# A float32 transformer with split weights: its memory pools opened in another order

## The chip, the cores and the metric

The kernel runs on one core of a Trainium2 chip. The metric is the device time of one execution in microseconds (us), the median of several runs.

## The reference

Two transformer blocks of two layers each work on one sequence of 256 tokens, 1024 features wide, in float32. The first block has in each layer a gated feed-forward, a mixer (window attention beside a gated convolution, then a gated recurrence) and a second gated feed-forward, each behind an RMS norm. The second block has norms that are scaled and shifted by a modulation, a mixer of three kinds of attention, and a dense feed-forward in its first layer; in its second layer a mixture of eight experts, of which each token takes two. Most of the arithmetic is the product of 256 tokens with large weights:

```python
def _swiglu(x, wg, wu, wd):
    return (jax.nn.silu(x @ wg) * (x @ wu)) @ wd      # wg, wu: 1024 x 2816, wd: 2816 x 1024
...
    for e in range(N_EXPERTS):
        out = out + gates[..., e:e + 1] * _swiglu_2(h, w_gate[e], w_up[e], w_down[e])
```

## The kernel before

**Products.** TensorE (PE) multiplies in float32r. To keep float32 accuracy, each operand is split into two float32r parts, a high one and a low one, and a product is the sum of three matmuls: high by high, low by high, high by low (`mm3`, lines 334, 335 and 337). In nearly all of them the activations, transposed, are the stationary operand (`lhsT`, 128 x 128, in a slot), and a row tile of a weight, 512 or 256 columns wide, is the moving operand (`rhs`). `fmajor` (line 595) has it the other way round: 128 columns of a weight are stationary, and both token tiles of the activations, 2 x 128 columns, move. The experts with few tokens put the two parts of 64 tokens side by side in one stationary operand, so that two matmuls do (line 429).

**Weights.** `load` (line 300) brings a piece of a weight, mostly 128 partitions x 2048 columns (1 MB), from DRAM into one of four `raw` tiles, on SP's queue. `split` (line 306) makes the two parts of each half of it: ScalarE (ACT) copies 1024 columns to a `wh` tile in float32r (by way of `act`, line 222), and VectorE (DVE) subtracts that from `raw` into a `wl` tile (by way of `tt`, line 231). There are eight `wh` and eight `wl` tiles of 4 KB per partition. In the feed-forwards of the first block and the dense one, one or two slots (`ext`) serve as a ninth and tenth pair. The feed-forwards go through their 2816 hidden columns in six chunks: up products of a chunk, the gate, the transpose of the hidden columns (line 457), the down products into accumulators `acc`.

**Pools.** `K.__init__` opens the pools one after the other, and each begins where the one before it ends. Every tile is rounded up to 32 bytes per partition. In the order of before:

- `cst`, the constants: `x0` and `x1` (4096 bytes per partition each), `ident` and `ones` (512 each), `fold` (32), `mhalf` (64), `cols` (1600), `consts` (3744), `sincos` (512), together 15168 bytes. It begins at byte 16512 = 129 x 128 of each partition.
- `raw`, four tiles of 8192 bytes; `wh` and `wl`, eight of 4096 bytes each.
- `sm`, small tiles of 4 to 512 bytes, together 5152 bytes.
- `slots`: `s8` of 4096 bytes and eleven more of 8192: activations, their split transposes, gains, hidden columns, attention.

Two pools outside SBUF follow, `ps` (PSUM) and `dr` (DRAM). Which tile serves which step, the order of the instructions and the queues are set by the rest of the program, which names pools and tags and no addresses.

**The experts** (`moe`): the tokens are sorted into seven places, the largest expert's chunks run beside the others' by a plan (`plan`), and 264 pieces of weights are loaded for them. `scatter` (line 1579) multiplies in plain float32.

Of the kernel before, what the change touches and what calls it, by code (L numbers as in the profile page):

```python
# [20 lines left out]
# where each chunk's parts begin in a packed feed-forward  # L21
# [4 lines left out]
# ---------------------------------------------------------------- host layout  # L26
# [63 lines left out]
def pack(inp):  # L90
    a = {}
# [4 lines left out]
    # even mixer: conv value and gate by halves, queries by pairs of heads that use different keys, keys and values  # L96
    w = inp["even_w_in"][0]
# [7 lines left out]
    # odd mixer: half of the gate, recurrence, the rest of the gate  # L105
    w = inp["odd_w_in"][0]
# [6 lines left out]
    # per-feature vectors, features on partitions  # L113
# [15 lines left out]
    r = inp["moe_router_2"][0]  # L129
# [3 lines left out]
    # per-feature vectors as rows  # L133
# [5 lines left out]
    # modulation: 6 segments of 1024 a layer, outputs on partitions  # L139
# [4 lines left out]
    # second mixer: [q latent, kv latent, rope key], [band q, band k], [stick q, stick k], [stick v, band v]  # L144
# [19 lines left out]
    # constants of the shapes  # L164
# [27 lines left out]
# ---------------------------------------------------------------- device  # L192
class K:
    def __init__(self, ctx, tc, A, out, dbg=None):
        self.tc, self.nc, self.A, self.out, self.dbg = tc, tc.nc, A, out, dbg or {}
        e = ctx.enter_context
        self.cst = e(tc.tile_pool(name="cst", bufs=1))
        self.raw_p = e(tc.tile_pool(name="raw", bufs=4))
        self.h_p = e(tc.tile_pool(name="wh", bufs=8))
        self.l_p = e(tc.tile_pool(name="wl", bufs=8))  # L200
        self.sm_p = e(tc.tile_pool(name="sm", bufs=1))
        self.slots = e(tc.tile_pool(name="slots", bufs=1))
        self.ps = e(tc.tile_pool(name="ps", bufs=4, space=bass.MemoryType.PSUM))
        self.dr = e(tc.tile_pool(name="dr", bufs=1, space=bass.MemoryType.DRAM))
        self.n = 0
        self.ext, self.turn, self.in_moe, self.c_row = (), 0, False, None
        self.first, self.behind = True, None
        self.setup()

    # --- small helpers  # L210
# [13 lines left out]
    def warm(self, func, after):  # L224
        """has the scalar engine load a function's table behind one of its instructions"""
        t = self.small("mx", 2, bufs=1)[:, 0:1]
        with self.tc.issue_after(after.ins):
            return self.act(t, self.ones[:, 0:1], func)
# [27 lines left out]
    def setup_late(self):  # L256
        """what the first products don't need"""
# [20 lines left out]
    def begin(self, ins):  # L278
        """the first norms' steps keep their order"""
        return self.pin(ins) if self.first else ins  # L280
# [16 lines left out]
    # --- weights: raw piece from DRAM, split exactly into two float32r parts  # L297
# [8 lines left out]
    def split(self, raw, nk, n, pin=False):  # L306
        """nk row tiles by n columns: a list over row tiles of the (hi, lo) views [128, n]"""
# [21 lines left out]
    def mm3(self, out, xs, ws, first, last):  # L329
        """out += x.T @ w over pairs; xs, ws lists of (hi, lo) operands"""  # L330
# [8 lines left out]
    def mm3_groups(self, out, xs, groups, c0, n, first, last):  # L339
        """the same over groups of row tiles, columns c0:c0 + n of each"""  # L340
# [6 lines left out]
    def rstd(self, ss, n, eps, tag="r"):  # L347
        """1 / sqrt(ss + eps)"""
# [17 lines left out]
    def stat(self, t, h, gain=None):  # L366
        """mean squares of one half of a token tile; with a gain, of the product too, which is kept"""
# [25 lines left out]
    def split_T(self, xT, t, src, groups=(0, 1)):  # L393
        """src [128 tokens, 1024] -> the two parts of its transpose, [128, token tile, 8, 128]"""
# [25 lines left out]
    # --- gated feed-forward  # L420
    def prod(self, out, xs, groups, c0, n, first, last, half=False):
        """out += x.T @ w. Half: the two parts of 64 tokens lie side by side in x, and their products land in
        the two halves of the partitions"""
# [20 lines left out]
    def glu_T(self, u, n, h, l, half=False):  # L444
        """the two parts of the transpose; of half a tile side by side in h"""
# [15 lines left out]
    def ffn(self, src, base, xk, tiles, finish, side=None, tick=None, ext=(), defer=None, hl=(2, 3), bufs=None, half=False, hook=None, head=None):  # L461
# [65 lines left out]
        def down_w(c):  # L527
            """groups of row tiles and their first column, for each half of the output"""
# [50 lines left out]
    # --- feature-major projection: columns of w on partitions, both token tiles in the free axis  # L579
    def fmajor(self, out, xT, groups, c0, n=128):  # L580
        """out [n, 256] = (x @ w[:, c0:c0 + n]).T"""
# [15 lines left out]
    def tmajor(self, out, xT, t, groups, c0, n):  # L597
        """out [128 tokens, n] = x @ w[:, c0:c0 + n]"""
# [3 lines left out]
    def in_block(self, src, off, n):  # L602
        """the row tiles of one block of n columns of a 1024-row weight"""
# [34 lines left out]
    # --- softmax attention of one query tile; score banks hold heads side by side  # L638
    def softmax_av(self, nk, banks, p_sb, pt_sb, values, o, rinv, sinks=None, scale=None):
        """banks: (psum view [128, heads, nk * 128], head ids); o [128, heads * 64] psum; rinv [128, heads]"""  # L640
# [39 lines left out]
    # --- first block, layer 0: window attention beside a gated convolution  # L680
    def even_mixer(self, xT, finish, defer):
        nc, A = self.nc, self.A
        src = A["ew_in"]
        # bias of each head by distance, skewed through DRAM: A[p, j] = r[p + j], p = 127 - query
# [20 lines left out]
        # keys and values, a token tile at a time  # L705
# [34 lines left out]
        # depthwise convolution over time  # L740
# [7 lines left out]
        # attention  # L748
# [26 lines left out]
        # the last channels by products with the taps on a diagonal  # L775
# [14 lines left out]
        # norm over channels, by sums over partitions that land on all of them  # L790
# [29 lines left out]
    def decay(self):  # L820
        """4 log sigmoid(lam), and its negative; halves of the gates' biases"""
# [26 lines left out]
    # --- first block, layer 1: gated linear recurrence  # L848
    def odd_mixer(self, xT, finish, defer):
# [9 lines left out]
        # half of the gate, a token tile at a time  # L859
# [12 lines left out]
        def gates(g, b):  # L872
            """twice the sigmoid less one"""
# [43 lines left out]
        def pre(b, n=1):  # L917
            sl = slice(2 * b, 2 * (b + n))
            # 1 - a^2 = tanh(-log a) (1 + a^2)
# [51 lines left out]
    # --- second block: modulation of both layers, spread over the first block's products  # L971
# [63 lines left out]
    def final_norm_mod(self, t, shift, gain, xT):  # L1035
        """the norm between the blocks, then the modulated one, of the product that stat kept"""
# [12 lines left out]
    def rope_tables(self):  # L1049
# [17 lines left out]
        for which, quarter in ((0, 0.0), (1, 0.25)):  # L1067
            # nearest whole turn, then the rest in three exact steps
# [10 lines left out]
        # [sin | sin] -> [-sin | sin]  # L1079
        self.ts(self.sc[:, 0, :, 0:16], self.sc[:, 0, :, 0:16], -1.0)  # L1080

    def rope(self, out, src, t, nh, tmp):
        """out, src [128, nh, 32]; src in psum"""
# [8 lines left out]
    def band_tables(self):  # L1092
        """band bias of both layers: edge value, then the table, in DRAM to be read skewed"""
# [9 lines left out]
    def mixer(self, l, xT, finish, defer):  # L1103
# [14 lines left out]
        # latents of the low-rank attention, normed, transposed  # L1118
# [11 lines left out]
        for t, p in enumerate(pa):  # L1130
# [13 lines left out]
            # the key part that turns, shared by the heads, and its share of their mean squares  # L1144
# [9 lines left out]
        # stick-breaking queries and keys, feature-major  # L1154
# [7 lines left out]
        # band attention's queries and keys: normed a head, transposed by pairs  # L1162
# [16 lines left out]
        # up-projections, rope, keys normed a head (a query's norm goes into the softmax's scale), transposes  # L1179
# [51 lines left out]
        # stick-breaking: keys on partitions; log weights are z - sum of softplus from the key up to the query  # L1231
# [29 lines left out]
        # values of both  # L1261
# [10 lines left out]
        def stick():  # L1272
            # the sums over the keys behind, the weights and their products with the values
# [28 lines left out]
        # band attention  # L1302
        def band(t):
# [13 lines left out]
            # places in order of (j, i); head 2 i + j  # L1317
# [7 lines left out]
        # low-rank attention  # L1325
# [49 lines left out]
    # --- experts: tokens gathered by one-hot products, 128 to a slot  # L1375
# [8 lines left out]
    def logits(self, t, xT):  # L1384
        """router logits of one token tile; the parts of the router side by side"""
# [8 lines left out]
    def moe(self, h, res, xT, defer):  # L1394
# [5 lines left out]
        # the first expert's first hidden columns, for every token: its products run beside the routing  # L1400
# [18 lines left out]
        # rank of each expert for a token: larger logit first, then lower index  # L1419
# [12 lines left out]
        # place of each token in its expert's list, from 1 (0: not in it), and the experts' counts on all partitions  # L1432
# [11 lines left out]
        def tables(one, kinds, pcol):  # L1444
            """one-hot of place by token for each token tile; kinds: the first place of each 128 rows, and whether
            they are 64 places twice, for the two parts"""
# [9 lines left out]
        def gather(one, kinds, outs, alone=False):  # L1456
            """the two parts of the gathered tokens, transposed; a half's side by side"""
# [23 lines left out]
        def turned(one, oneT, nb, gcol):  # L1481
            """the one-hots transposed, and each place's gate"""
# [13 lines left out]
        def make(got, i, m, half, pcol, gcol):  # L1496
            """fills got with what an expert's slot needs; m has room for the one-hots and their transposes"""
# [29 lines left out]
        # expert 0 has the first slot; the others follow by count: room for 192 tokens, 128 (three) and 64 (three)  # L1527
# [13 lines left out]
        # one-hot [slot, expert]  # L1541
# [21 lines left out]
        # tokens that no slot has room for  # L1563
# [8 lines left out]
        def scatter(parts):  # L1572
            """parts of the product that carries places back to tokens, added to x"""
# [9 lines left out]
        def expert(src, got, out, **kw):  # L1583
            """the tokens of one slot"""
# [17 lines left out]
        # the expert with the most tokens: 128 and 64 more, a chunk of its products beside each later expert's  # L1602
# [78 lines left out]
        def head():  # L1681
            """the places' part of the first hidden columns, transposed"""
# [10 lines left out]
        # when each chunk of the largest expert is done: most beside the experts of 64  # L1693
# [58 lines left out]
def emit(tc, A, out, dbg=None):  # L1752
    with ExitStack() as ctx:
# [6 lines left out]
        def prep(name):  # L1760
            """the norm in front of a part, for one token tile at a time"""
# [94 lines left out]
# ---------------------------------------------------------------- launch  # L1856
# [15 lines left out]
```

## Time and profile before

| | |
|---|---|
| median of 3 runs | 2288.79 us |
| lowest and highest | 2286.12 and 2289.21 us |
| span of the profiled execution (first to last instruction) | 2284.9 us |
| what the median of the runs has beyond that span | 3.9 us |
| PE busy | 98% of the span, 10976 matmuls |
| DVE busy | 75% |
| ACT busy | 58% |
| read from DRAM | 569.8 MB, 250 GB/s over the span |

The profile names a group of instructions by source line, engine and operation, then what is written and read by the program's names (`mm<-wh,s`: a PSUM tile, written from a moving operand in `wh` and a stationary one in a slot). For a matmul the first name behind the arrow is the moving operand. The profile writes f32 for float32 and for PE's float32r alike. A matmul's end is modelled, and matmuls overlap in it; the distance from one start to the next is measured.

### The profile page before, as it was taken

To read this page: it belongs to the slowest core of one execution; us is meant where nothing else is said; L and a number is where in the kernel's file an instruction comes from. 1 tells how busy PE (TensorE), PEld (TensorE's weight loads), DVE (VectorE), ACT (ScalarE), POOL (GpSimd) and SP (SyncE) were. 2 spreads that over 40 slices of the span, in tenths; PEclk is the share of its full clock that TensorE was granted. 3 is DMA by queue.
4 is the path that set the end of the run, shared out by engine and by line. 5 is a ranking of instruction groups with operands and counts; after the bars stand their busy time and mean duration, and the time that the engine had idled before them with its cause. 6 is when DMAs were issued, how large, how long until landed. Compare 5 with 4: busy or idle time off the path is not lost.

```text
span 2284.9 us, 29602 instructions
## 1 busy us (share of the span) xinstructions
PE 2228.5 (98%) x10976; PEld 1807.9 (79%) x10976; DVE 1720.4 (75%) x2205; ACT 1333.9 (58%) x1819; POOL 94.6 (4%) x152
## 2 busy tenths in 40 slices
PE   8999999999999999999999999999999999999998
PEld 6888878888888788887788878887788776877676
DVE  6785967658656876575754666889988999889996
ACT  6445554444436744456544475677766777767764
POOL 0001000000000100030100121000000000000000
PEclk9999999999999999999999999999999999999999
DMA  8784258658764587533555342688988888988886
GB/s 335 261 313 163 102 184 310 251 193 303 255 236 144 193 312 266 202 139 129 212 184 181 127 172 106 247 332 338 342 325 320 319 331 319 338 333 331 328 319 235
DMA packets 82263, 572.92 MB, mean 251 GB/s; under 512 B 9373, under 2 KB 9685, under 8 KB 15424
## 3 DMA queue, kind: packets, MB, share of 16 engines
q1 hardware_dynamic: 77616, 556.73, 66.1%
q0 software_dynamic: 3920, 13.12, 1.7%
q8 instruction: 88, 1.44, 0.3%
q10 hardware_dynamic: 576, 1.11, 0.1%
q14 instruction: 63, 0.52, 0.1%
HBM read 569.80 MB, written 1.12 MB: 250 GB/s over the span
## 4 chain that ended last, share of the span: by engine, by line
PE 49%; DVE 4%; ACT 2%; issue 1%; POOL 0%; DMA 0%; ACTq 0%; DVEq 0%; POOLq 0%
PE mm L334 7%; PE mm L335 7%; PE mm L337 7%; PE mm L429 6%; PE acc L335 4%; PE acc L337 4%; PE acc L334 4%; PE acc L429 3%; DVE wl L231 3%; PE mm L1579 1%; ACT wh L222 1%; PE mm L1467 1%; DVE s L231 1%; PE mm L595 1%; PE mm L676 1%
## 5 line engine op out<-in xcount | busy, mean ns | idle before, releaser
L231 DVE TENSOR_TENSOR wl<-raw,wh 128x1024 fp32r<-128x1024 f32 (+1 forms) x908 | 1078.6, 1216 | 283.8 <-ACT wh L222 279.1
L222 ACT ACTIVATE wh<-raw 128x1024 fp32r<-128x1024 f32 (+1 forms) x908 | 920.2, 1052 | 377.9 <-PE mm L335 165.4
L334 PE MATMUL mm<-wh,s 128*128 128x512 f32 (+2 forms) x1384 | 521.1, 382 | 3.3 <-ACT s L222 3.2
L335 PE MATMUL mm<-wh,s 128*128 128x512 f32 (+2 forms) x1384 | 516.4, 378 | 1.0 <-DVE s L231 1.0
L222 ACT ACTIVATE s<-mm 128x512 fp32r<-128x512 f32 (+7 forms) x387 | 199.8, 533 | 367.0 <-PE mm L337 100.8
L337 PE MATMUL mm<-wl,s 128*128 128x512 f32 (+2 forms) x1384 | 402.6, 378 | 0.6 <-DVE wl L231 0.5
L334 PE MATMUL acc<-wh,s 128*128 128x512 f32 x788 | 315.2, 401 | 3.6 <-DVE s L231 1.8
L335 PE MATMUL acc<-wh,s 128*128 128x512 f32 x788 | 313.4, 398 | 2.3 <-DVE s L231 2.3
L334 PEld LDWEIGHTS mm<-wh,s 128*128 128x128 f32 x1384 | 260.3, 188 | 56.9 <-ACT s L222 4.9
L335 PEld LDWEIGHTS mm<-wh,s 128*128 128x128 f32 x1384 | 260.8, 188 | 54.2 <-DVE s L231 3.4
L337 PEld LDWEIGHTS mm<-wl,s 128*128 128x128 f32 x1384 | 249.0, 188 | 53.4 <-DVE wl L231 1.7
L337 PE MATMUL acc<-wl,s 128*128 128x512 f32 x788 | 254.9, 396 | 0.6 <-DVE wl L231 0.5
L334 PEld LDWEIGHTS acc<-wh,s 128*128 128x128 f32 x788 | 148.3, 188 | 38.5 <-DVE s L231 3.0
L335 PEld LDWEIGHTS acc<-wh,s 128*128 128x128 f32 x788 | 148.5, 188 | 35.7 <-DVE s L231 3.7
L337 PEld LDWEIGHTS acc<-wl,s 128*128 128x128 f32 x788 | 147.5, 188 | 36.1 <-DVE wl L231 2.2
L429 PE MATMUL mm<-wl,s 128*128 128x512 f32 (+1 forms) x384 | 145.4, 385 | 2.9 <-DVE wl L231 2.7
L231 DVE TENSOR_TENSOR s<-mm,s 128x512 fp32r<-128x512 f32 (+5 forms) x216 | 128.7, 619 | 21.7 <-ACT s L222 20.6
L429 PE MATMUL mm<-wh,s 128*128 128x512 f32 (+1 forms) x384 | 144.6, 384 | 0.0
L987 DVE SCALAR_TENSOR_TENSOR raw<-raw,s 128x1024 f32<-128x1024 f32 x96 | 114.3, 1220 | 3.4 <-ACT s L222 1.7
L231 DVE TENSOR_TENSOR s<-s,mm 128x512 f32<-128x512 f32 (+1 forms) x93 | 59.7, 642 | 54.5 <-PE mm L337 48.4
L222 ACT ACTIVATE s<-raw 128x1024 fp32r<-128x1024 f32 x50 | 52.7, 1064 | 71.6 <-PE mm L337 33.5
L429 PEld LDWEIGHTS mm<-wl,s 128*128 128x128 f32 x384 | 72.6, 189 | 23.4 <-DVE wl L231 9.0
(308 smaller groups left out, 2182.9 us busy)
## 6 DMA issues: line engine op xcount, KB each, us to landing
raw<-in_moe SPq DMA_DIRECT2D x264, 1024.0 KB, 5.3
raw<-in_f SPq DMA_DIRECT2D x132, 1024.0 KB, 6.2
raw<-in_ada_w SPq DMA_DIRECT2D x48, 1024.0 KB, 5.0
raw<-in_dense SPq DMA_DIRECT2D x33, 1024.0 KB, 4.9
raw<-in_w_in SPq DMA_DIRECT2D x12, 1024.0 KB, 4.9
raw<-in_ow_in SPq DMA_DIRECT2D x8, 1024.0 KB, 4.9
raw<-in_w_out SPq DMA_DIRECT2D x8, 1024.0 KB, 5.2
raw<-in_ew_in SPq DMA_DIRECT2D x7, 1024.0 KB, 4.9
```

The costliest lines, as they stand in the source:

```text
L222: return self.nc.scalar.activation(out=out, in_=in_, func=func, **kw)
L231: return self.nc.vector.tensor_tensor(out=out, in0=in0, in1=in1, op=op)
L334: mm(out=out, lhsT=xs[i][0], rhs=ws[i][0], start=first and i == 0, stop=False)
L335: mm(out=out, lhsT=xs[i][1], rhs=ws[i][0], start=False, stop=False)
L337: mm(out=out, lhsT=xs[i][0], rhs=ws[i][1], start=False, stop=last and i == n - 1)
L429: self.nc.tensor.matmul(out=out, lhsT=x[0], rhs=w[j][:, c0:c0 + n], start=first and k == 0 and j == 0, stop=last and k == len(ws) - 1 and ...
L595: mm(out=out, lhsT=a, rhs=b, start=j == 0, stop=j == len(todo) - 1)
L676: nc.tensor.matmul(out=o[:, hd * 64:(hd + 1) * 64], lhsT=pt_sb[:, (i * nk + kb) * 128:(i * nk + kb + 1) * 128], rhs=values(kb, hd), start= ...
L987: self.nc.vector.scalar_tensor_tensor(out=src, in0=src, scalar=1.0, in1=self.c_row, op0=OP.mult, op1=OP.mult, accum_out=p[:, 2 * pc + i:2 ...
L1467: mm(out=p[:, k * w:(k + 1) * w], lhsT=h[t][:, a, kk * 128:(kk + 1) * 128], rhs=one[:, o:o + w], start=t == 0, stop=t == 1)
L1579: mm(out=p, lhsT=o[:, t * 128:(t + 1) * 128], rhs=v[:, sl], start=b == 0, stop=b == len(parts) - 1)
```

## The change

It opens the three weight pools first, then the slots, and the constants behind them, ahead of the small tiles. Sizes, numbers of buffers and all else of the program stay. The rest of the diff takes comments and docstrings out.

```diff
         e = ctx.enter_context
-        self.cst = e(tc.tile_pool(name="cst", bufs=1))
         self.raw_p = e(tc.tile_pool(name="raw", bufs=4))
         self.h_p = e(tc.tile_pool(name="wh", bufs=8))
         self.l_p = e(tc.tile_pool(name="wl", bufs=8))
+        self.slots = e(tc.tile_pool(name="slots", bufs=1))
+        self.cst = e(tc.tile_pool(name="cst", bufs=1))
         self.sm_p = e(tc.tile_pool(name="sm", bufs=1))
-        self.slots = e(tc.tile_pool(name="slots", bufs=1))
         self.ps = e(tc.tile_pool(name="ps", bufs=4, space=bass.MemoryType.PSUM))
         self.dr = e(tc.tile_pool(name="dr", bufs=1, space=bass.MemoryType.DRAM))
```

The first of the weight pools then begins at byte 16512 = 129 x 128, where the constants began. `raw`, `wh`, `wl` and the slots take 192512 = 1504 x 128 bytes together, and each of their tiles is a multiple of 128 bytes long.

## Rows read from the trace of the kernel before

**Rows 1.** The page, busy time, share of the span and instructions of each engine.

```profile
PE 2228.5 (98%) x10976; PEld 1807.9 (79%) x10976; DVE 1720.4 (75%) x2205; ACT 1333.9 (58%) x1819; POOL 94.6 (4%) x152
```

**Rows 2.** Two stretches: busy us per engine (instructions), granted clock, DMA share, GB/s.

```profile
core 0: us, PE busy (x) PEld busy (x) DVE busy (x) ACT busy (x) POOL busy (x), PEclk, DMA share, GB/s
0.00:1459.00 1459.00, 1429.20 (x7247) 1180.33 (x7248) 989.77 (x1429) 748.34 (x1127) 94.58 (x152) 1.00 0.58 210
1459.00:2285.00 826.00, 799.27 (x3731) 627.58 (x3729) 730.62 (x777) 585.60 (x693) 0.00 (x0) 1.00 0.86 322
```

**Rows 3.** Chain of waits, 1459 us to the end, shares by line.

```profile
by line: PE mm L429 15.2%; PE mm L334 11.9%; PE mm L337 11.9%; PE mm L335 11.8%; PE acc L429 7.4%; DVE wl L231 6.4%; PE acc L337 5.9%; PE acc L335 5.8%; PE acc L334 5.8%; PE mm L1579 3.8%; ACT wh L222 3.0%; issue 2.7%; PE mm L1467 1.9%; DVE
```

**Rows 4.** Groups on PE: count | busy us, mean ns of one | idle before.

```profile
L334 PE MATMUL mm<-wh,s 128*128 128x512 f32 x1144 | 457.3, 400 | 1.1 <-ACT s L222 1.0
...
L334 PE MATMUL acc<-wh,s 128*128 128x512 f32 x780 | 313.0, 402 | 3.6 <-DVE s L231 1.8 <-ACT s L222 1.7
...
L429 PE MATMUL mm<-wl,s 128*128 128x512 f32 x320 | 129.6, 405 | 2.9 <-DVE wl L231 2.7
...
L429 PE MATMUL acc<-wl,s 128*128 128x512 f32 x176 | 71.6, 411 | 3.2 <-DVE wl L231 2.9
...
L334 PE MATMUL mm<-wh,s 128*128 128x256 f32 x208 | 52.3, 285 | 0.0
```

**Rows 5.** Timeline of PE from 399 us: start us, length us, instruction, count.

```profile
399.71 0.39 PE L335 MATMUL acc<-s,s 128*128 128x512 f32 x1
...
401.75 0.61 PE L337 MATMUL acc<-s,s 128*128 128x512 f32 x2
402.21 0.40 PE L334 MATMUL acc<-wh,s 128*128 128x512 f32 x1
...
405.71 0.40 PE L335 MATMUL acc<-wh,s 128*128 128x512 f32 x1
```

**Rows 6.** Groups on ACT and DVE, same columns as rows 4.

```profile
L222 ACT ACTIVATE wh<-raw 128x1024 fp32r<-128x1024 f32 x896 | 909.6, 1054 | 366.7 <-PE mm L335 157.2 <-PE acc L335 127.8 <-DMA raw<-in_moe 29.7
...
L222 ACT ACTIVATE s<-raw 128x1024 fp32r<-128x1024 f32 x50 | 52.7, 1064 | 71.6 <-PE mm L337 33.5 <-PE acc L337 21.5 <-issue 8.6
...
L231 DVE TENSOR_TENSOR s<-s,s 128x512 f32<-128x512 f32 x16 | 10.3, 684 | 0.0
...
L231 DVE TENSOR_TENSOR x<-x,s 128x512 f32<-128x512 f32 x12 | 8.2, 687 | 0.2
```

**Rows 7.** Transfers: count, KB each, median us from issue to landing.

```profile
s<-in_c SPq DMA_DIRECT2D x4, 512.0 KB, 5.1
...
x<-in_x SPq DMA_DIRECT2D x2, 512.0 KB, 5.2
```

**Rows 8.** Chain of waits from 2190 us: start us, us, what.

```profile
2198.38 6.87 PE mm L1579 x16
```

**Rows 9.** Timeline of PE from 480 us, matmuls of 256 columns.

```profile
480.13 0.28 PE L334 MATMUL mm<-wh,s 128*128 128x256 f32 x1
...
482.97 0.28 PE L334 MATMUL mm<-s,s 128*128 128x256 f32 x1
...
485.37 0.40 PE L337 MATMUL mm<-s,s 128*128 128x256 f32 x2
```

**Rows 10.** Line 595: a piece of the chain, and its count before 1459 us.

```profile
1000.53 8.89 PE mm L595 x76
...
0.00:1459.00 1459.00, 92.08 (x768) 1.00 0.58 210
```

**Rows 11.** Groups on PE behind 1459 us, same columns as rows 4.

```profile
L334 PE MATMUL mm<-wh,s 128*128 128x512 f32 x378 | 151.8, 402 | 0.0
...
L334 PE MATMUL acc<-wh,s 128*128 128x512 f32 x220 | 88.8, 405 | 1.1 <-ACT s L222 1.0
```

**Rows 12.** Waits behind 1459 us: who for whom, us, times, longest.

```profile
DVE wl L231 <- ACT wh L222: 47.7, 77, 2.9
...
ACT wh L222 <- DMA raw<-in_moe: 29.7, 31, 2.4
```

## Prediction

> **What bounds the kernel now.** I read first the busy shares [rows 1]: PE is busy for 98% of the 2284.9 us span, DVE for 75%, ACT for 58%. Of a pipelined engine "busy" does not say how dense its work is, so I then took the span in two: before 1459 us (feed-forwards and mixers) PE is busy for 1429 of 1459 us with the DMA engines at 0.58 and DVE at 990 us; behind it (the experts) for 799 of 826 us, with the DMA engines at 0.86 and DVE at 731 us; the granted clock is 1.00 in both, the 2.4 GHz level [rows 2]. So the first 1459 us hang on PE with room on every feeder, and the experts on PE with DVE and the DMA close behind. The chain of waits says the same of the experts: the PE entries of its line sum to 81%, DVE's `wl` is 6.4%, ACT's `wh` 3.0% [rows 3]. (The whole chain can be traced back only to about 988 us, so I don't use it for the first part.)
>
> What PE does there is mostly one form, 512 columns of float32r (the profile writes f32) with the moving operand in `wh` or `wl`: 3 x 1144 + 3 x 780 + 2 x 320 + 2 x 176 = 6764 of its 10976 matmuls [rows 4]. (Lines 334, 335 and 337 have equal counts, line 429 one group for `wh` and one for `wl`.) Some of this form have the moving operand in a slot `s`, where the feed-forwards keep every ninth and tenth weight tile.
>
> The third reading decides the case: not the durations but the distance from one matmul's start to the next one's, in one stretch where both kinds stand side by side on one accumulator [rows 5]. With the moving operand in `s`: 399.71 to 401.75 us in 9 steps, **226.7 ns** each. With it in `wh`/`wl`: 402.21 to 405.71 in 15 steps, **233.3 ns** each. Nothing waits in either run, the stationary operand is in a slot in both, the number of columns is the same. What differs is where the moving operand lies. From the sizes declared: the constants begin at a multiple of 128 bytes and take 15168 = 118 x 128 + 64 bytes, so every `raw`, `wh` and `wl` tile begins 64 bytes past a multiple of 128 (their sizes are multiples of it); `sm` takes 5152 = 40 x 128 + 32 more, so every slot begins 96 past one. Column blocks of 512 and 256 keep that offset.
>
> **The change part by part.** No instruction is added, removed or issued elsewhere; sizes and buffer counts stay, so I take the order on every engine and queue to stay, SP's and POOL's too. What changes: `raw`, `wh`, `wl` go from offset 64 to 0, slots from 96 to 0. Constants and `sm` come behind 192512 = 1504 x 128 bytes, so their offsets stay.
>
> *ACT and DVE*: nothing. ACT's half of the split takes 1054 ns at 64 and 1064 ns into a slot at 96; an addition on DVE 687 ns into `x`, whose offset is 0 already, and 684 ns from slot to slot [rows 6]. The offset doesn't show there beyond 1%, and the side at 0 is no faster.
>
> *Transfers*: nothing. 512 KB into `x` (0) lands in 5.2 us, into a slot (96) in 5.1 us [rows 7].
>
> *Matmuls of 512 columns*: no row has this form with its moving operand at offset 0, so I bound it. Below: the plain float32 matmuls of line 1579 take 6.87/16 = 429 ns for 512 columns, 0.84 ns a column or two periods of the clock [rows 8]; half of that, **214.7 ns**, is an estimate of a stream with one period a column in which nothing is lost. Above: one more step of the size that separates the two offsets, 233.3 + 6.6 = **239.9 ns**. I take 226.7 ns, for the row that is nearest: in the slot rows both operands have one offset (96 and 96), in the `wh` rows they have two (64 and 96). The change gives them one offset again, and if the loss is a clash of the moving stream with the weight load beside it, only their distance counts. The short forms point the same way, to two operands rather than one: with 256 columns both at 96 give 2.40/20 = 120.0 ns, 64 with 96 gives 2.84/24 = 118.3 [rows 9], and 96 moving with 64 stationary (line 595) 8.89/76 = 117.0 [rows 10].
> The Trainium skill (TensorE: Matmul & The Clock Gate, "Back-to-back issue gap") gives N/2.4 + 2.5 ns for a warm stream, 215.8 for 512 columns, and no word on addresses; rows 8 agree with it at two periods a column (429.2), rows 5 do not (226.7 and 233.3). By it every 512-column step could come down to 215.8 whatever the address, and the sum would be that of the first rival, 2189 us; by rows 5 it is 2251.
>
> *The sum.* Of the 6764 matmuls, 3 x 378 + 3 x 220 and all of line 429, 2786 in sum, lie behind 1459 us [rows 4, 11], so 3978 before. Before: 3978 x 6.6 ns = 26.2 us, all of it on the path, since no feeder is near its limit. Experts: 2786 x 6.6 = 18.4 us, of which I count the chain's PE share, 0.81: 14.9 us; the rest meets what is late next, DVE's `wl` behind ACT (47.7 us of waits) and ACT behind the experts' loads (29.7 us) [rows 12]. The forms of 256 columns lose by the same rule: 3 x 208 with `wh`/`wl` moving go from 118.3 to 120.0 (1.1 us) [rows 4], 768 of line 595 from 117.0 to 120.0 (2.3 us) [rows 10]. Together -26.2 - 14.9 + 3.4 = -37.7 us on the 2284.9 us span; the median of the runs, 2288.79, is 3.9 us above it, so 2251 us. If the experts gave nothing it would be 2266; if they gave all, 2248.
>
> **The rivals.**
> *Full alignment (0.27).* The loss is that of each operand's own offset, and at 0 none is left: 214.7 ns. Before the experts 3978 x 18.6 ns = 74 us. The experts could give 2786 x 18.6 = 52 us; with DVE at 731 us and 48 us of waits in 826 us [rows 2, 12], I count half, 26. Sum 100: **2189 us**, 2215 if the experts give nothing, 2163 if they give all. For it: beyond the floor, offset 64 loses more with more columns (233.3 - 214.7 = 18.6 ns at 512, 118.3 - 107.4 = 10.9 at 256), which a weight load of fixed length doesn't explain. Against: offset 64 is the rounder of the two and yet the slower.
>
> *No change (0.15).* It isn't the offset but the place: `wh` and `wl` lie below the slots, and still do afterwards. Then 233.3 stays and the time is **2289 us**. For it: offset and pool go together in every row. The Trainium skill (SBUF — State Buffer, "Specifications") speaks for it too: SBUF lines are 16 bytes, and 0, 64 and 96 are all multiples. By that rule no offset here matters; rows 5 show a difference all the same, though not which of the two makes it.
>
> *Slower (0.15).* Equal offsets put the first lines of both streams of every matmul onto each other, and at 0 they clash more than at 96; in the 256-column rows the equal pair is the slowest already [rows 9]. Price at the upper bound: 6764 x 6.6 = 44.6 us, all on the path as PE then bounds everything, with 3.4 us for the short forms: **2337 us**. It decides as soon as the `wh` step is above 233.3 ns.
>
> That the change doesn't do what it says I exclude: the first weight tile takes the place of the first constant, at a multiple of 128.
>
> **How the numbers follow.** The forecast has 0.43, with a range of its own of 2243 to 2266. Faster is forecast plus full alignment: 0.70; same 0.15; slower 0.15. I call same what is within 0.2%, 4.6 us, about what a measurement here can tell from nothing. The range leaves out the slower case and the lowest end of full alignment: 2175 to 2292, its upper end 3 us above no change.
>
> **What would show it.** In the profile after, a `wh` run of line 334/335 should step by 227 ns (right), by 215 to 220 (full alignment), by 233 (place), or above (slower); line 595 should go from 117 to 120 ns. ACT's and DVE's means should stay within 1%, and the experts' waits on `wl` and on the loads should grow by a few us. I am wrong if the 512-column step stays or rises, or if the steps fall and the span doesn't follow.

## The result and the profile after

| | before | after |
|---|---|---|
| median of 4 runs each | 2289.0 us | **2260.2 us** |
| lowest and highest | 2286.12 and 2294.48 us | 2258.82 and 2264.67 us |
| span of the profiled execution | 2284.9 us | 2258.0 us |

The ratio of after to before is **0.9878**, 95% interval 0.9864 to 0.9893: 28.8 us faster. The forecast was 2251 us: right in direction and in the kind of step, and 9 us too low.

The page first, the line that answers to [rows 1]:

```profile
PE 2200.2 (97%) x10976; PEld 1812.7 (80%) x10976; DVE 1719.0 (76%) x2205; ACT 1336.0 (59%) x1819; POOL 92.9 (4%) x152
```

PE has 28.3 us less of busy time with the same 10976 matmuls. DVE and ACT have what they had. The two stretches of [rows 2], cut at 1441 us, which is the same place of the program (the first product of the experts has moved from 1449.40 to 1431.81 us):

```profile
core 0: us, PE busy (x) PEld busy (x) DVE busy (x) ACT busy (x) POOL busy (x), PEclk, DMA share, GB/s
0.00:1441.00 1441.00, 1410.34 (x7245) 1183.67 (x7246) 989.07 (x1429) 748.36 (x1126) 92.94 (x152) 1.00 0.58 213
1441.00:2258.00 817.00, 789.86 (x3733) 629.07 (x3731) 729.91 (x777) 587.61 (x693) 0.00 (x0) 0.99 0.87 326
```

The timeline of PE at the accumulator of [rows 5] (start us, length us, instruction, count):

```profile
394.70 0.39 PE L335 MATMUL acc<-s,s 128*128 128x512 f32 x1
...
396.74 0.39 PE L334 MATMUL acc<-wh,s 128*128 128x512 f32 x1
...
398.10 0.39 PE L334 MATMUL acc<-wh,s 128*128 128x512 f32 x1
...
400.82 0.39 PE L334 MATMUL acc<-wh,s 128*128 128x512 f32 x1
```

With the moving operand in a slot it takes 9 steps from 394.70 to 396.74 us, 226.7 ns each, as before. With it in `wh`/`wl` it takes 18 steps from 396.74 to 400.82, 226.7 ns each, where [rows 5] had 233.3. The two kinds are now alike. A piece of line 595 in the chain of waits, and a group of 256 columns, answer to [rows 10] and to the last of [rows 4]:

```profile
986.76 9.12 PE mm L595 x76
```

```profile
L334 PE MATMUL mm<-wh,s 128*128 128x256 f32 x208 | 52.8, 286 | 0.0
```

9.12/76 = 120.0 ns, from 117.0: the small loss that the forecast had too. ACT's split has the mean of before, 1054 ns [rows 6], and line 1579's 16 float32 matmuls take 6.87 us again [rows 8]:

```profile
L222 ACT ACTIVATE wh<-raw 128x1024 fp32r<-128x1024 f32 x896 | 910.4, 1054 | 360.1 <-PE mm L335 144.3 <-PE acc L335 122.0 <-DMA raw<-in_moe 29.5
```

```profile
2172.92 6.87 PE mm L1579 x16
```

All 10975 steps from one matmul's start to the next can be paired between the two traces, since the order on PE is the same. Sorted by what they are (a *break* is a step of a 512-column product that is longer than 260 ns in either trace or ends at a product with another number of columns; a *row* is what lies between two breaks, products that move a slot included), and cut at the first product of the experts:

```
                                 ahead of the experts          experts
512 columns, wh/wl moving       steps    mean ns    us      steps    mean ns    us
  eleventh step of a row on     3135  233.3->226.7 -20.9    1623  233.3->226.7 -10.8
  first ten steps of a row       623  232.7->229.6  -2.0     871  232.9->230.5  -2.1
  break                          202  376.4->383.4  +1.4     310  355.4->363.3  +2.5
256 columns                                         +3.1                        +0.7
all else                                            +0.4                        +0.6
sum                                                -18.0                        -9.2
```

Together -27.1 us; the span fell by 26.9.

Not every break is a wait. Nine of the experts' 310, +1.6 of their +2.5 us, lie in one stretch in which the granted clock was 0.50, the 1.2 GHz level, and most of the steps took 426 to 428 ns. Four more, +0.6 us, stand behind one late transfer in the chain of waits. First the stretch (same columns as [rows 2]), then the transfer:

```profile
1626.63:1630.04 3.41, 3.41 (x10) 2.67 (x9) 3.41 (x4) 1.61 (x2) 0.00 (x0) 0.50 0.73 243
```

```profile
1586.08 8.85 DMA raw<-in_moe
```

Shortly before the clock fell, PE had waited 0.80 and 0.74 us for DVE. While PE works on the experts, the trace after has two such stretches of 3.4 us and the trace before has one; ahead of the experts each has two.

### The profile page after: what moved, and what is told of

It is laid out like the page before. It is cut to its first block, busy times and chain, and to the rows that moved or that the text cites. A ratio compares the mean times of both kernels' runs of the same rounds, so it can differ in the third digit from the quotient of the medians.

```text
span 2258.0 us, 29602 instructions
## 1 busy us (share of the span) xinstructions
PE 2200.2 (97%) x10976; PEld 1812.7 (80%) x10976; DVE 1719.0 (76%) x2205; ACT 1336.0 (59%) x1819; POOL 92.9 (4%) x152
## 4 chain that ended last, share of the span: by engine, by line
PE 46%; DVE 5%; ACT 3%; issue 2%; DMA 1%; POOL 1%; ACTq 0%; DVEq 0%; POOLq 0%
PE mm L334 7%; PE mm L335 7%; PE mm L337 7%; PE mm L429 5%; PE acc L335 4%; PE acc L334 4%; PE acc L337 4%; DVE wl L231 3%; PE acc L429 2%; ACT wh L222 2%; PE mm L1579 1%; ACT s L222 1%; DVE s L231 1%; PE mm L595 1%; PE mm L1467 1%
## 5 line engine op out<-in xcount | busy, mean ns | idle before, releaser
L334 PE MATMUL mm<-wh,s 128*128 128x512 f32 (+2 forms) x1384 | 515.9, 378 | 3.2 <-ACT s L222 3.2
L335 PE MATMUL mm<-wh,s 128*128 128x512 f32 (+2 forms) x1384 | 511.1, 374 | 1.0 <-DVE s L231 1.0
L337 PE MATMUL mm<-wl,s 128*128 128x512 f32 (+2 forms) x1384 | 396.1, 374 | 0.2
```

What stands on the lines that cost most here:

```text
L334: mm(out=out, lhsT=xs[i][0], rhs=ws[i][0], start=first and i == 0, stop=False)
L335: mm(out=out, lhsT=xs[i][1], rhs=ws[i][0], start=False, stop=False)
L337: mm(out=out, lhsT=xs[i][0], rhs=ws[i][1], start=False, stop=last and i == n - 1)
```

## The experiments

Three theories stood at the start, the first in two forms. *Distance*: the step depends on how far the moving and the stationary operand lie from each other. The forecast's form of it was that the step is short when the two have the same offset from a multiple of 128. *Full multiple*: being at a multiple of 128 is what counts. *Place*: the low or high part of the memory, or where the constants lie.

**A grid of offsets.** Four moving and four stationary tiles stand 0, 32, 64 and 96 bytes past a multiple of 128, and every pair makes a row of products (in the diffs of the small kernels the comments are added):

```diff
+ for n in (512, 256):
+     for m in "abcd":
+         for s in "abcd":
+             p = run(m, s, n, 128)      # 24 matmuls: moving tile m, stationary tile s
```

> This kernel leaves out the whole computation: it runs rows of 24 products of one moving and one stationary tile, for all sixteen pairs of tiles that begin at 0, 32, 64 and 96 bytes past a multiple of 128, at 512 and at 256 columns, and then four pairs with 64 and with 32 stationary columns. Theory of equal offsets (the forecast): the four pairs with equal offsets step at about 227 ns at 512 columns, the twelve others at about 233 ns, whatever the absolute offset. Theory of the full multiple: the pair with both at 0 alone is below the others, near 215 to 227 ns, and the pair 96 with 96 is like any other pair. Theory of the place in the memory: no pair differs from another by more than 1 ns. If it is the load of the next stationary tile that the moving columns meet, the loss of the unequal pairs shrinks with the stationary columns, to about a half at 64 and a quarter at 32; if it is a cost at the start of each matmul, it stays at 6 ns.

Four of its rows of 24 products at 512 columns, each from its first start to that of the next row (a stretch: us, PE busy; the 25th product is a neighbour that overlaps the end):

```profile
core 0: us, PE busy (x), PEclk, DMA share, GB/s
23.07:28.64 5.57, 5.57 (x25) 1.00 0.01 3
28.64:34.24 5.60, 5.60 (x25) 1.00 0.00 0
34.24:39.74 5.50, 5.50 (x25) 1.00 0.00 0
50.96:56.53 5.58, 5.58 (x25) 1.00 0.01 3
```

They are 0 with 0, 0 with 32, 0 with 64 and 32 with 32 (moving with stationary): 5.57/24 = 232.1 ns, 233.3, 229.2 and 232.5. All four pairs of equal offsets stood between 232.4 and 233.4 ns from their fourth step on, and the two lowest pairs (228.8) were 0 with 64 and 32 with 96. So the forecast's rule is wrong as it was put, and so is the full multiple. But pairs of one distance (first address of the stationary tile less that of the moving one, past a multiple of 256 bytes) agree: three at 160 have 233.4, three at 96 have 234.2 to 234.4, the two at 192 have 228.8. And in this kernel all pairs of equal offsets lie an odd multiple of 128 bytes apart. The rows with 64 and 32 stationary columns gave 226.7 to 232.7 and 230.2 to 233.4 ns, with no order in them; whether the loss shrinks with the stationary columns stays open.

**A sweep of the distance.** One moving tile, and a stationary one that begins 32 bytes further in each row:

```diff
+ for r in range(0, 256, 8):
+     run([(0, r)])                      # columns of 4 bytes: 0 to 992 bytes
+ walk = lambda m, s: [(m + 512 * (k % 4), s + 128 * k) for k in range(8)]
...
+ for r in (0, 8, 16, 24, 32, 64):
+     run([(0, r)], 256)                 # 256 columns
+ for r in (1, 2, 4):
+     p = run([(0, r)])                  # 4, 8 and 16 bytes
```

> This kernel leaves out the whole computation: it runs rows of 24 products from one moving and one stationary block; the distance between their first addresses grows from 0 by 32 bytes to 992 (one pair repeated), then stands at 0, 32, 64, 96, 128, 256, 384 and 512 bytes while the stationary tiles walk 512 bytes and the moving ones 2048 bytes from product to product as in the kernel, then both are shifted alike by 32, 64, 96 and 128 bytes. The first grid had 232.4 to 233.5 ns for four pairs of equal offsets (their distance was 128 past a multiple of 256) and 228.9 for two pairs at 192 past a multiple of 256, so equal offsets in a line of 128 bytes are not enough by themselves. Theory of the distance over a longer period: the step is a function of the distance that repeats after 256 or 512 bytes, and the walk at distance 0 gives about 227 ns, at 32 bytes 233 ns, at 128 bytes again 232 to 233 ns; shifting both alike leaves 227. Theory of equal offsets in 128 bytes: the walk gives 227 at 0, 128, 256, 384 and 512 and 233 at 32, 64 and 96. Theory of the full multiple: shifting both alike by 32 to 96 bytes gives 233 and by 128 gives 227. Theory of the place: all within 1 ns.

The rows at 0, 32, 64, 96, 128, 160, 192, 224 and 256 bytes, in this order, 24 products each, same columns as above:

```profile
23.32:28.76 5.45, 5.45 (x25) 1.00 0.01 3
28.76:34.35 5.59, 5.59 (x25) 1.00 0.00 0
34.35:39.95 5.60, 5.60 (x25) 1.00 0.00 0
39.95:45.56 5.61, 5.61 (x25) 1.00 0.00 0
45.56:51.16 5.60, 5.60 (x25) 1.00 0.00 0
51.16:56.77 5.60, 5.60 (x25) 1.00 0.01 3
56.77:62.27 5.51, 5.51 (x25) 1.00 0.00 0
62.27:67.87 5.59, 5.59 (x25) 1.00 0.00 0
67.87:73.32 5.45, 5.45 (x25) 1.00 0.00 0
```

From the fourth step on the rows have **226.7 ns at 0, 228.8 at 192, 233.3 to 234.4 at the six others**, and 256 bytes on the same values come again, through to 992. Walking as the kernel does changes little: 226.7 at 0, 233.4 at 32, 233.3 at 64, 234.4 at 96, 233.3 at 128, 227.9 at 256, 232.4 at 384, 226.7 at 512. Shifting both operands alike by 32, 64, 96 or 128 bytes gives 227.7 in all four cases, so the offset by itself does nothing. (The means of 227.7 and 227.9 hold first steps of 224 to 236 ns; from the ninth step on all these rows stand at 226.7.) In the sweep only the stationary tile's address differs between rows; the moving tile stays, the accumulator bank of the rows at 0 and 128 is the same, and the other engines are idle. What is left for the moving stream to meet is the load of the stationary tile. That is an argument and not shown: the rows with fewer stationary columns, meant to test it, gave no answer.

**Four kernels, four distances.** Since `wh` and `wl` are multiples of 256 bytes long, one number tells a kernel's distance. Before the change `sm` with its 5152 = 20 x 256 + 32 bytes stood between weights and slots: 32. Now nothing does: 0. The next four put other distances into the whole kernel. The first undoes the distance and keeps all else of the change (in this kernel, the second and the fourth, tiles of the last branch share a buffer, to make room; those lines are left out):

```diff
- self.l_p = e(tc.tile_pool(name="wl", bufs=8))
+ self.l_p = e(tc.tile_pool(name="wl", bufs=8)); e(tc.tile_pool(name="gap", bufs=1)).tile([128, 8], F32, name="gap")
```

> The changed kernel with the slots alone moved 32 bytes on: weights stay at a multiple of 128 and the pools in their new order, slots stand 32 bytes past a multiple of 128, and the distance of slots and weights is 32 past a multiple of 256 as before the change. Theory of the distance (period 256, grids above: 226.7 at 0, 233.3 at 32): 512-column products step at 233.3 ns again and the time is that of the kernel before, 2287 to 2291 us. Theory of the place or the pool order: 2260 us. Theory of weights at a multiple of 128 as what counts: 2260 us.

Measured: **2288.51 us**, ratio to before 0.9993 (0.9981 to 1.0005). The gain is gone, with the pools in their new order and the weights at multiples of 128, and the settled 512-column steps are back at 233.3 ns. The second has a gap of 128 bytes there, so that weights and slots both stay at multiples of 128:

> The changed kernel with the slots moved 128 bytes on: weights and slots both still at multiples of 128, as the change wants, but the distance is 128 past a multiple of 256. Theory of the distance with a period of 256 bytes (233.3 ns at 128 in the grid): the gain is gone, 2284 to 2291 us. Theory of equal offsets in 128 bytes, the forecast's own, and theory of the full multiple of 128: 2260 us, steps of 227 ns.

Measured: **2289.28 us**, ratio 0.9996 (0.9984 to 1.0008). The same accumulator in its timeline:

```profile
401.43 0.40 PE L334 MATMUL acc<-wh,s 128*128 128x512 f32 x1
...
405.62 0.40 PE L334 MATMUL acc<-wh,s 128*128 128x512 f32 x1
```

18 steps in 4.19 us, 232.8 ns. What the change does by its own words, each tile at a multiple of 128 bytes, brings nothing. The third is the kernel before, its pools in the old order, with 32 bytes less in `sm`; this is its whole edit:

```diff
- now = self.small("now", 8, bufs=1)
+ now = self.small("lu", 8, bufs=1)
```

> The kernel before in its old pool order with 32 bytes less of small tiles ahead of the slots (a tile of the last branch shares a buffer): weights and slots are both 64 bytes past a multiple of 128, none at a multiple, constants at their old place, and the distance is 0 past a multiple of 256. Theory of the distance: the whole gain of the change, 2258 to 2264 us, steps of 227 ns. Theory of multiples of 128 and theory of the new places or of the constants' place: 2289 us, steps of 233 ns.

Measured: **2260.29 us**, ratio 0.9865 (0.9843 to 0.9887): the whole gain, from one line that moves the slots down by 32 bytes. Its timeline has 18 steps in 4.08 us, 226.7 ns:

```profile
396.45 0.39 PE L334 MATMUL acc<-wh,s 128*128 128x512 f32 x1
...
400.53 0.39 PE L334 MATMUL acc<-wh,s 128*128 128x512 f32 x1
```

No tile of the weights or slots is at a multiple of 128 in it, and the constants are where they were. Place and full multiple fall with this run, equal offsets in 128 bytes with the one before it. The fourth asks whether the size follows too, at the one distance with a step between the two:

```diff
+ self.slots = e(tc.tile_pool(name="slots", bufs=1))
- self.raw_p = e(tc.tile_pool(name="raw", bufs=4))
+ gap = e(tc.tile_pool(name="gap", bufs=1)); self.raw_p = e(tc.tile_pool(name="raw", bufs=4))
  self.h_p = e(tc.tile_pool(name="wh", bufs=8))
- self.l_p = e(tc.tile_pool(name="wl", bufs=8))
+ self.l_p = e(tc.tile_pool(name="wl", bufs=8)); gap.tile([128, 16], F32, name="gap")
- self.slots = e(tc.tile_pool(name="slots", bufs=1))
```

> The changed kernel with the slots ahead of the weights and a gap of 64 bytes between them: weights stand 64 bytes past a multiple of 128, slots at a multiple, and the distance is 192 past a multiple of 256, the one other distance that the grid had below 233 (228.8 ns). Theory of the distance: about two thirds of the gain stay ((233.3 - 228.8) / (233.3 - 226.7) = 0.68 of 28 us), 2266 to 2275 us. Theory of equal offsets in 128 bytes, and of multiples of 128: none of it, 2289 us.

Measured: **2267.86 us**, ratio 0.9921 (0.9899 to 0.9944). Its span is 2265.4 us, 19.5 below that of before, 0.72 of the 26.9 us that the change gained, for 0.68 expected. Its settled 512-column steps average 229.0 ns.

**Who took part of the experts' gain.** The forecast let 0.81 of it through and put the rest down to late weights. Two kernels with half of the experts' transfers test that; in the experts every second piece is split from the raw block of the piece before it:

```diff
+ raw, self.again = (self.again, None) if self.again else (self.raw_p.tile([128, 2048], F32, tag="raw", name="raw"),) * 2
+ if self.again: self.nc.sync.dma_start(out=raw[:, :n], in_=src[off:off + 128 * n].rearrange("(p n) -> p n", p=128))
+ self.again = self.again if self.in_moe and n == 2048 else None; return raw
```

> The kernel before with every second transfer of expert weights left out: the next piece is split from the same raw block, so half of the experts' bytes do not come and the output is another. It measures, with its counterpart of the changed kernel, who swallowed part of the experts' gain (9.3 us found of 2786 products by 5.9 ns = 16.4). If the weight stream holds the experts (DMA share 0.86 there), this kernel is 10 to 26 us faster than the kernel before (26.7 us of TensorE's time were idle there); if it does not, it is within 5 us of it.

> The changed kernel with the same half of the expert transfers left out. Theory that the stream swallowed the rest: the gap to its counterpart with the old pool order grows from 26.9 to 32 to 35 us, with 15 to 17 us of it behind the first expert product. Rival, that the rest is lost in the short rows of products themselves, whose first steps stand between 229 and 236 ns until the pattern settles: the gap stays at 26 to 29 us, with 9 to 11 us of it behind the first expert product.

Measured: 2280.38 us (ratio to before 0.9965, 0.9951 to 0.9979) and 2252.4 us (0.9838, 0.9822 to 0.9855). The program orders some instructions otherwise than in the full kernels, alike in both of the pair. The experts' stretch of the two, from their first product on:

```profile
1449.40:2277.30 827.90, 806.63 (x3797) 641.91 (x3795) 743.13 (x816) 605.96 (x701) 0.64 (x1) 0.99 0.45 161
```

```profile
1432.70:2251.30 818.60, 795.62 (x3797) 642.83 (x3795) 742.21 (x816) 605.90 (x701) 0.64 (x1) 0.99 0.46 163
```

The DMA share is halved, 0.86 to 0.45, and the experts' gain is what it was: 827.9 - 818.6 = **9.3 us**, for 835.5 - 826.2 = 9.3 in the full kernels. (In both pairs the changed kernel has 3.4 us more at the 1.2 GHz level in the experts than its counterpart, so that doesn't set the pairs apart.) But for the 0.6 us behind the late transfer, the stream did not swallow it. That the light kernel before is 7.8 us faster lies between what the two theories had for it; PE's waits on `wh` and `wl` in the experts fell from 10.0 to 3.2 us with the old pool order and from 10.3 to 3.3 with the new one: a cost beside the change, not one that it meets. DVE's subtractions were not lightened (743 of 828 us), so of DVE alone this says nothing.

**Do rows have to settle?** The table of steps above says where much of the experts' gain stays: in the first ten steps of a row, where 871 products gave 2.1 us instead of 871 x 6.6 ns = 5.7. A small kernel makes short rows by itself, without transfers and with idle engines beside it:

```diff
+ for r in range(0, 64, 8):              # distances 0, 32, ... 224 bytes
+     for i in range(4):
+         # four passes of a float32 product (or a wait for ACT), then 16 products
+         p = run(walk(0, r), rep=16)
```

> This kernel leaves out the whole computation: it runs rows of 16 products (tiles walk as in the kernel) at distances of 0, 32, ... 224 bytes, 4 rows each, first each behind two float32 products, then each behind a wait for ScalarE. In the changed kernel's experts the first two steps of a row average 232.7 ns, the fifth and sixth 230.6, and from about the eleventh on 226.7; the kernel before stands at 232.5 to 233.4 throughout. Theory that a row has to settle: at distance 0 the first eight steps average 229 to 233 ns and steps 11 to 15 stand at 226.7, behind either kind of break, and at 32 all stand at 232 to 234. Rival, that the slow first steps belong to something else in the experts (weights that arrive late, other engines' work): at distance 0 all steps stand within 1 ns of 226.7 from the second step on.

A row at distance 0 and one at 32, with the breaks around them (timeline of PE):

```profile
32.02 0.60 PE L46 MATMUL mm<-raw 128*128 128x128 f32 x4
32.38 3.89 PE L36 MATMUL mm<-mv,st 128*128 128x512 f32 x16
36.10 0.60 PE L46 MATMUL mm<-raw 128*128 128x128 f32 x4
...
40.19 0.60 PE L46 MATMUL mm<-raw 128*128 128x128 f32 x4
40.55 3.97 PE L36 MATMUL mm<-mv,st 128*128 128x512 f32 x16
44.36 0.61 PE L46 MATMUL mm<-raw 128*128 128x128 f32 x4
```

The first row is 3.72 us from its first start to the next break, the second 3.81. The 15 steps of single rows in ns, out of the trace:

```
behind float32,   0: 314 233 230 227 227 226 227 227 226 227 227 226 227 227 226
behind float32,  32: 319 231 235 232 235 232 235 231 235 232 235 232 235 231 235
behind a wait,    0: 335 235 233 236 224 231 236 228 233 231 226 227 227 226 227
behind a wait,    0: 337 236 228 233 231 226 227 227 226 227 227 226 227 227 226
behind a wait,   32: 340 231 235 232 235 232 235 231 235 232 235 232 235 231 235
behind a wait,  192: 342 231 232 226 229 232 226 229 231 226 229 232 226 229 232
```

Rows settle. Past the first step, at distance 0 it takes two steps behind float32 products in all four rows; behind a wait it takes nine in one row and four in the three others. They start as high as a row at 32. At 32 the steps never leave 229 to 235. The expectation had not counted the first step, which holds the break itself (314 to 342 ns); with it the first eight average 238.8 and 243.5, without it 228 to 230. In the kernel settling takes about ten steps, near the longest of these rows; what sets the length was not tried.

## Why the prediction was right, point by point

- **What bounds the kernel, and the step**: right. The 512-column step fell to 226.7 ns, the forecast's value, in every row that has settled, and 595's rose to 120.0. It is the relation of two operands, as [rows 5, 9, 10] let the forecast argue, and full alignment, place and the clash at 0 did not come (no step at 215, none left at 233.3 in the long rows, none at 240).
- **The rule behind it**: only half right. "Only their distance counts" holds; "the change gives them one offset again" is not enough. Equal offsets 128 bytes apart step at 233. It came out well by luck: `wh` and `wl` together are 65536 = 256 x 256 bytes, so that the distance is 0 past a multiple of 256 as well.
- **3978 x 6.6 = 26.2 us before the experts**: this term was too large. Of 3960 products 3135 got 6.7 ns shorter, but 623 stand among the first ten of a row and got 3.2 shorter, and 202 end in a break and got 7 longer: 20.9 + 2.0 - 1.4 = 21.5 us. The forecast read its step from one long row and gave it to each product.
- **14.9 us in the experts**: the term that failed most, 10.8 + 2.1 - 2.5 = 10.4 us. At 6.6 ns each, its 2804 products would have given 18.5. Of the 8.1 us that are missing, 3.6 are missing in the first ten steps of rows (871 of 2804 products, against 623 of 3960 ahead of the experts) and 4.5 in the breaks (310, against 202). Of those 4.5, 2.0 are steps that did not get shorter and 2.5 steps that got longer, 1.6 of these at the lower clock and 0.6 behind the late transfer. So the share of 0.81 was the right kind of caution with, in the main, the wrong cause: of the late weights that the forecast named, 0.6 us and little more show, and the clock it had not counted at all. PE's waits for `wh` and `wl` went from 10.0 to 10.3 us. The waits behind 1441 us that answer to [rows 12] hardly moved, where the forecast had them grow by a few us:

```profile
DVE wl L231 <- ACT wh L222: 46.1, 63, 2.7
...
ACT wh L222 <- DMA raw<-in_moe: 29.5, 35, 2.0
```

- **+3.4 us for 256 columns**: right, 3.1 + 0.7 = 3.8.
- **Nothing on ACT, DVE and the transfers**: right for ACT and DVE. The experts' transfers went from 5.3 to 5.6 us each; the pair with half of them gained the same 9.3 us, so that took no more from the change than the 0.6 us above.
- **The sum**: -26.2 - 14.9 + 3.4 = -37.7 forecast; -21.5 - 10.4 + 3.8 and 1.0 of other forms = -27.1 found. The measured time lies in the forecast's own range, 2243 to 2266; the wider one had been set by the first rival (2189 us), which no run came near.

Two rules bear on this. The Trainium skill (TensorE: Matmul & The Clock Gate, "Step-by-step: what each phase is for") says that loading the next weights takes no read bandwidth from the running matmul; the sweep does not agree that the two are independent, since there the address of the stationary tile alone moves the step from 226.7 to 234.4 ns. Whether it is read bandwidth that is lost, no run shows. The Trainium skill (SBUF — State Buffer, "Specifications") gives 16-byte lines, and by that no multiple of 16 should matter; steps at distances of 4, 8 and 16 bytes were 232.2, 230.7 and 233.3 ns, and the period that shows is 256 bytes. The formula behind the forecast's 215.8 ns stands in the section that the forecast names (the Trainium skill, TensorE: Matmul & The Clock Gate, "Back-to-back issue gap") as the gap of an isolated matmul and not of a stream; no 512-column row here settled below 226.6 ns.

## What to carry to other kernels

Where PE streams matmuls that each have their own weight load, look at start-to-start steps and at the addresses of both operands: here a distance of 0 past a multiple of 256 bytes between moving and stationary tiles was worth 6.6 ns of 233 in each 512-column float32r product of a settled row, and one small pool between them, 32 bytes too long, cost 1.2% of the kernel. Being at a multiple of 128 was worth nothing. Price such a gain from long and short rows apart: a row after a break gets it only once it has settled. Other data types were not tried.

## What the runs showed of the hardware that was not expected

- The step depends on the distance with a period of 256 bytes, and not monotonically: 226.7 ns at 0, 228.8 at 192, 233.3 to 234.4 at 32, 64, 96, 128, 160 and 224. Why 192 is better than 64 is open, as is what in the memory has this period.
- At 256 columns it is the other way round: 120.0 ns at 0, 118.3 at 32, 117.8 at 64, 117.4 at 96 in the sweep. In the grid some pairs of one distance differed there (64: 113.4 and 117.8), so distance alone doesn't tell that form.
- At settled distance 0 the step is still 226.7 ns, above the 214.7 that the forecast worked out as the floor from line 1579. No row of the grid, of the sweep or of the short rows settled below 226.6 at 512 columns, and no version of the kernel with shorter steps was run.
- TensorE's granted clock fell to 0.50 for 3.4 us at a time in the middle of the kernel, once in the experts before the change and twice after it. The additional stretch took 1.6 us of the gain. The kernel in the old order with 32 bytes less in `sm`, with the same gain, has it at the same place (1626.5 us), the one with the gap of 32 bytes, without the gain, has it not; what sets it off is open.
